# Loading order of the MLP weights in a decoder layer: the block that is added to comes first

## The chip, the cores and the metric

The kernel runs on one core of one Trainium2 chip. The core has a matmul engine (TensorE, PE in the profile, with PEld for its weight loads), a vector engine (VectorE, DVE), a scalar engine (ScalarE, ACT), GpSimd (POOL) and SyncE (SP). Each takes its instructions in the order in which they were written down and waits on semaphores for the others. PE accumulates in PSUM; everything else lies in SBUF. Transfers between HBM and SBUF are issued by SP or POOL and carried by 16 DMA engines. The metric is the device time of one execution in microseconds (us).

## The reference, cut to what matters

A hybrid layer: a chunked mLSTM and a sliding-window attention on one normalised input, an output projection, an MLP, a gated extra embedding and a last norm. 512 tokens, width 1024, float32. What the change touches is the MLP with its 4096 hidden features:

```python
u = rmsnorm(x, norm_mlp_g[i]) @ w_up[i]
x = x + jnp.square(jax.nn.relu(u)) @ w_down[i]
```

## The kernel before

**Arithmetic.** A float32 number is split into two parts of the type float32r: the high part is a rounded copy, made by ACT (a cast, L1318), and the low part is what the copy lost, made by DVE (a subtraction, L1321). A product is three matmuls, high by high, high by low and low by high. One pair of parts of a 128 x 1024 block of weights is called a form here; there are four buffers of each part (`wh`, `wl`), so a form waits until the product four forms earlier has been computed.

**Seven products for eight.** Most of the MLP is done as 2 x 2 blocks by Winograd's form of Strassen's method: seven block products, w1 to w7, and some sums of blocks. The weights of one such set are four blocks b11, b12, b21, b22 (for the down projection two of each, one for each half `kh` of the contracted features). The sums on the weights' side are made in place:

- t3 = b12 + b22. It is made by a transfer: b12 is loaded, and then POOL issues a second transfer of b22 from HBM that adds to the same buffer while it arrives (`add_to`, L1299). This is called the adding transfer. b22 is also loaded by itself.
- t2 = t3 - b11, written over b11 (DVE, L1559 in an up set, L1648 in the down projection), t4 = b21 - t2 over b21, t1 = b22 - t2 over b11 (DVE, L1563, L1564, L1648).

So b11 serves w1, then t2 takes its place for w6, then t1 for w5; t3 serves w7, b22 w3, and b21 first w2 and then, as t4, w4. The order of the products on PE is w1, w2, w6, w5, w7, w3, w4, in the first down projection w2 before w1.

**Order of the stages.** The first eight 128-row pieces of the up projection are computed plainly (`up_first`). Then follow: down 0; up set 2, up set 3, down 1; up set 4, up set 5, down 2; up set 6, up set 7, down 3. An up set (L1485 on) gives 512 hidden features, a down projection (L1592 on) takes 1024 of them. Between one stage and the next PE has no pause by itself: the first product of the next stage is written directly behind the last one of this stage.

**Results.** In an up set w2's sum plus a copy k1 of w1 becomes one quarter (called c11), w7's sum plus a copy becomes c22, w3's c12; these additions are DVE's L1544, followed by ACT's ReLU and square. Three accumulators X, Y, Z in PSUM are reused: w4 is written on X and must wait until c22 has read it. In a down projection DVE adds each finished accumulator to the residual stream `xk` (L1631); the last two of these additions read Y, which the next up set's w2 overwrites.

**Two rings of buffers.** Raw blocks land in two rings of four buffers each, `wr` and `wd`. A load may start when the block that had this buffer four loads earlier in the same ring has had its last reader (`ring_free`), and loads of a ring start in order. Even up sets use `wr`, odd ones `wd`. A down projection uses both: `wr` for b11 and b21, `wd` for b12 and b22.

**The plan.** `Plan.run` (L51 on) writes down the order of all engines' work from the tuples of `Plan.add`: engine, cost, dependencies, and `late`, the time from the task's end until another engine can use its result. Backwards from PE's order each task gets a due time; forwards the task that can begin first is written next, the earlier due one on a tie. Costs and `late` are estimates in us; for a load on SP 1.3 and 2.5, for an adding transfer on POOL 1.2 and 5.0. They decide nothing but the order. The loads of a set are created in the order b11, b21, b12, b22 (L1491, L1593), the adding transfer behind w1.

Of the kernel before, what the change touches and what calls it, by code (L numbers as in the profile page):

```python
# [13 lines left out]
ALU = mybir.AluOpType  # L14
# [67 lines left out]
def block_kernel(  # L82
# [30 lines left out]
    nc = tc.nc  # L113
# [247 lines left out]
    e1, _ = early_part(1)  # L361
# [75 lines left out]
    with tc.issue_after(copied.ins):  # L437
        xn2, _ = norm(2)
# [3 lines left out]
    for m in range(NT):  # L442
        if m == 1:
            columns(2, xn2)
        elif m == 2:
            with tc.issue_after(on_scalar):
                xn, _ = norm(3)
            _, on_vector = columns(3, xn)
# [4 lines left out]
        t = sp.tile([P, 256], F32, tag="vs", bufs=4, name=nm("vs"))  # L453
# [146 lines left out]
    for m in range(NT):  # L600
        t = tp_.tile([P, NH * (DV + 2)], F32R, tag="tk", bufs=4, name=nm("vm")).rearrange("p (h d) -> p h d", h=NH)
# [313 lines left out]
    for u in range(16):  # L915
# [4 lines left out]
        if u % 4 == 3:  # L920
            kp, n, _ = units[u]
# [104 lines left out]
    t2 = [None] * 8  # L1026
# [262 lines left out]
    plan = Plan(tc)  # L1289
    LO, HI, HALF_UP, HALF_DOWN = 1.15, 0.98, 1.45, 1.37  # L1290
    forms, ring, slots = [], {"wr": [], "wd": []}, {}

    def ring_free(tag):
        old = ring[tag]
        return old[-1:] + (slots["last", old[-4]] if len(old) > 3 else [])

    def add_to(t, src, user):

        return plan.add("POOL", 1.2, lambda: [nc.gpsimd.dma_start(out=slots[user], in_=src, accum_op=ALU.add)], [t], 5.0)  # L1299

    def load(tag, src, user):

        def go():
            slots[user] = (wr if tag == "wr" else wd)()
            return [nc.sync.dma_start(out=slots[user], in_=src)]

        t = plan.add("SP", 1.3, go, ring_free(tag), 2.5)
        ring[tag].append(t)
        slots["last", t] = []
        return t  # L1310
# [174 lines left out]
    def up_set(i, ready):  # L1485
# [2 lines left out]
        role[:] = [Y, Z, X]  # L1488
        tag = "wr" if i % 2 == 0 else "wd"
        name = [(i, n) for n in ("b11", "b21", "b12", "b22")]  # L1490
        l11, l21, l12, l22 = [load(tag, w_upb[4 * i - 8 + n], u) for u, n in zip(name, (0, 2, 1, 3))]  # L1491
        b11, b21, b12, b22 = name
        keep = {}

        def half(ps):
# [59 lines left out]

        begun_set = plan.add("none", 0, lambda: begin() or [], done_with.get("F", []) + done_with.get(("uf", i), []))
        w1 = prod(X, A11, b11, [l11], True, False, (done_with.get(id(X), []), []))
        t3 = add_to(l12, w_upb[4 * i - 8 + 3], b12)
        t2 = vec(LO, lambda: V.tensor_sub(slots[b11], slots[b12], slots[b11]), [t3, w1["lo"]])  # L1559
        w2 = prod(Y, A12, b21, [l21], True, True, (done_with.get(id(Y), []), []))  # L1560
        k1 = kept("k1", X, w1["use"], done_with.get("k1", []))
# [28 lines left out]
    uf_of = {}  # L1590

    def down(q, ready):  # L1592
        names = ("b11", "b21", "b12", "b22")  # L1593
        src = {
            (n, kh): ("wr" if i < 2 else "wd", w_down[q * 8 + 4 * kh + (0, 2, 1, 3)[i]], (q, n, kh, "d"))
            for i, n in enumerate(names)
            for kh in range(2)
        }
        ld = {k: load(*v) for k, v in src.items()}
        raw = lambda n, kh: slots[q, n, kh, "d"]  # L1600
        X, Y, Z = role
        Gb = G1_
# [43 lines left out]

        n2 = range(2)
        sub = lambda o, a, b: lambda: V.tensor_sub(raw(*o), raw(*a), raw(*b))  # L1648
        w1, w2, w6, w5, t1, t2, t3, t4 = [[None] * 2 for _ in range(8)]
        more = None  # L1650
        for kh in range(2):
            if not q:
                w2[kh], u2 = half(X, A12, "b21", kh, ld["b21", kh], True, True)
            w1[kh], u1 = half(Gb, A11, "b11", kh, ld["b11", kh], q == 0, False)
            t3[kh] = add_to(ld["b12", kh], w_down[q * 8 + 4 * kh + 3], (q, "b12", kh, "d"))
            t2[kh] = vec(LO, sub(("b11", kh), ("b12", kh), ("b11", kh)), [t3[kh], w1[kh]["lo"]])
            if q == 3 and kh == 1:
                more = acc(Gb, 1, 0, u1)
            if q:
                w2[kh], u2 = half(X, A12, "b21", kh, ld["b21", kh], True, True)  # L1660
# [266 lines left out]
```

## Time and profile before

| what | us |
|---|---|
| three runs, median (lowest to highest) | 879.85 (876.97 to 879.88) |
| the profiled execution, time | 878.63 |
| its span, from the first to the last instruction | 876.8 |
| stretch before `up_first` (0 to 488) | 488.0, PE busy 485.9 |
| `up_first` (488 to 526) | 38.0, PE busy 38.0 |
| down 0 to down 3 (526 to 816) | 290.0, PE busy 278.1, DVE busy 251.8 |
| embedding gate and last norm (816 to the end) | 60.8, PE busy 53.7 |

Busy PE time takes the modelled ends of overlapping matmuls, so a pause of PE is some 0.16 us longer between the starts of two matmuls than the idle time that a row gives in brackets. In the rows of the timeline the columns are: start, duration, engine, line, operation, output<-inputs by the program's names with buffer numbers left out, shape, count; in square brackets the idle time of the engine before it and what ended it. SPq and POOLq are the issuing of transfers. `xk<-psp` is an addition to the residual stream, `k<-psp,k` one of c11, c22, c12, `wl<-wr,wh` a low part, `wr<-wr,wr` or `wr<-wd,wr` a sum of blocks.

### The profile page before, as it was taken

The numbers are of one execution on the slowest core, as the hardware profiler recorded it, in microseconds if no ns is written. First come the engines' busy times: TensorE is split into PE (matmuls) and PEld (weight loads), VectorE is DVE, ScalarE is ACT, GpSimd is POOL, SyncE is SP. The second block draws the span as 40 slices with busy tenths as digits, with TensorE's granted clock in tenths as the row PEclk, the third lists the DMA queues.
The fourth block names the chain that finished last, engine by engine and source line by source line (L and its number), as shares of the span: only waits on it lengthen the run. The fifth ranks groups of instructions, "written<-read, shape, count | busy, mean of one in ns | idle before, by whom it ended". The sixth has DMA issues, their size and how long they took to land.

```text
span 876.8 us, 12755 instructions
## 1 busy us (share of the span) xinstructions
PE 855.7 (98%) x4854; PEld 739.6 (84%) x4854; DVE 716.9 (82%) x1028; ACT 522.1 (60%) x893; POOL 58.6 (7%) x89
## 2 busy tenths in 40 slices
PE   9999999999999999999999999999999998999996
PEld 7888789998877778888888887899889888987886
DVE  7898978774788889677896888799969996999657
ACT  6776656554676677844343766277427743764743
POOL 3221111000000000000020000000000000010000
PEclk9999999999999999999999999999999999999998
DMA  8677236435122165663243450825253545443402
GB/s 285 210 195 273 96 123 214 163 127 192 49 96 73 61 228 217 211 254 135 73 97 120 121 166 25 216 97 144 91 150 120 121 145 118 144 123 104 159 1 96
DMA packets 37391, 123.60 MB, mean 141 GB/s; under 512 B 5197, under 2 KB 5197, under 8 KB 37330
## 3 DMA queue, kind: packets, MB, share of 16 engines
q1 hardware_dynamic: 28578, 95.77, 31.9%
q0 software_dynamic: 8608, 26.75, 12.3%
q8 instruction: 38, 0.62, 0.3%
q10 hardware_dynamic: 144, 0.26, 0.1%
q14 instruction: 23, 0.19, 0.1%
HBM read 106.51 MB, written 11.54 MB: 135 GB/s over the span
## 4 chain that ended last, share of the span: by engine, by line
PE 63%; DVE 14%; issue 9%; DMA 8%; ACT 5%; POOL 0%; POOLq 0%; ACTq 0%; DVEq 0%
PE psg L222 25%; PE psa L222 10%; PE psp L1333 7%; PE psg L1333 6%; PE psp L222 6%; DVE wl L1321 5%; DMA wr<-in_w_upb 4%; PE pst L222 4%; DMA wd<-in_w_down 2%; DVE wr L1648 2%; DVE xk L1631 2%; ACT wh L1318 1%; PE psp L1167 1%; PE pst L899 1%; DMA wr<-in_w_down 1%
## 5 line engine op out<-in xcount | busy, mean ns | idle before, releaser
L183 ACT CAST wh<-wr 128x1024 fp32r<-128x1024 f32 x87 | 91.7, 1055 | 87.2 <-PE psg L222 29.9
L184 DVE TENSOR_TENSOR wl<-wr,wh 128x1024 fp32r<-128x1024 f32 x87 | 106.1, 1221 | 42.7 <-ACT wh L183 42.4
L1333 PE MATMUL psp<-x,wh 128*128 128x256 f32 x672 | 123.2, 286 | 8.8 <-DVE xk L1631 5.7
L1318 ACT CAST wh<-wr 128x1024 fp32r<-128x1024 f32 x67 | 69.5, 1049 | 92.0 <-DVE wr L1648 34.0
L1333 PEld LDWEIGHTS psp<-x,wh 128*128 128x128 f32 x672 | 106.1, 194 | 10.2 <-issue 6.2
L1333 PE MATMUL psp<-wh,uf 128*128 128x512 f32 x336 | 105.8, 390 | 0.3 <-ACT wh L1318 0.3
L1333 PE MATMUL psp<-x,wl 128*128 128x256 f32 x336 | 95.7, 285 | 0.0
L1321 DVE TENSOR_TENSOR wl<-wr,wh 128x1024 fp32r<-128x1024 f32 x67 | 81.1, 1221 | 6.0 <-ACT wh L1318 6.0
L222 PE MATMUL psg<-h,wh 128*128 128x512 f32 x256 | 80.1, 393 | 0.0
L1333 PEld LDWEIGHTS psp<-wh,uf 128*128 128x128 f32 x336 | 63.1, 188 | 14.3 <-ACT wh L1318 1.0
L1333 PE MATMUL psp<-wl,uf 128*128 128x512 f32 x168 | 65.9, 392 | 2.8 <-DVE wl L1321 2.8
L1333 PEld LDWEIGHTS psp<-x,wl 128*128 128x128 f32 x336 | 65.2, 194 | 0.0
L222 PEld LDWEIGHTS psg<-h,wh 128*128 128x128 f32 x256 | 46.9, 188 | 8.9
L222 PE MATMUL psg<-h,wl 128*128 128x512 f32 x128 | 50.1, 391 | 0.0
L1321 DVE TENSOR_TENSOR wl<-wd,wh 128x1024 fp32r<-128x1024 f32 x37 | 44.8, 1220 | 1.3 <-ACT wh L1318 1.1
L1318 ACT CAST wh<-wd 128x1024 fp32r<-128x1024 f32 x37 | 38.0, 1049 | 11.4 <-PE psp L1333 11.4
L1333 PEld LDWEIGHTS psp<-wl,uf 128*128 128x128 f32 x168 | 31.5, 188 | 10.6 <-DVE wl L1321 4.3
L222 PE MATMUL psg<-yb,wh 128*128 128x512 f32 x128 | 40.2, 394 | 0.2 <-issue 0.2
L1351 DVE TENSOR_TENSOR uf<-F,uf 128x512 fp32r<-128x512 f32 (+2 forms) x30 | 34.2, 1149 | 7.5 <-ACT uf L1350 7.2
L1631 DVE SCALAR_TENSOR_TENSOR xk<-psp,r,xk 128x512 f32<-128x512 f32 x42 | 30.0, 747 | 11.2 <-PE psp L1333 11.0
L1333 PE MATMUL psg<-wh,uf 128*128 128x512 f32 x112 | 36.5, 389 | 0.0
L222 PE MATMUL psg<-ya,wh 128*128 128x512 f32 x112 | 34.9, 391 | 0.0
(401 smaller groups left out, 2150.7 us busy)
## 6 DMA issues: line engine op xcount, KB each, us to landing
wr<-in_w_down SPq DMA_DIRECT2D x16, 512.0 KB, 4.5
wd<-in_w_down SPq DMA_DIRECT2D x16, 512.0 KB, 4.3
wr<-in_w_upb SPq DMA_DIRECT2D x12, 512.0 KB, 3.5
wd<-in_w_upb SPq DMA_DIRECT2D x12, 512.0 KB, 4.4
wr<-in_w_qsw SPq DMA_DIRECT2D x8, 512.0 KB, 4.3
gd<-gr POOLq DMA_DIRECT2D x8, 512.0 KB, 3.5
wr<-in_w_qkml SPq DMA_DIRECT2D x8, 512.0 KB, 3.2
wr<-in_w_b SPq DMA_DIRECT2D x8, 512.0 KB, 3.5
```

The lines of the kernel that those rows point to most:

```text
L183: A.copy(dst[0], src)
L184: last_low[0] = V.tensor_sub(dst[1], src, r32(dst[0]))
L222: last_mm[0] = T.matmul(ps, l, r, start=first and i == 0, stop=last and i == len(ops) - 1, skip_group_check=parts)
L899: T.matmul(o[HALF[ab], :], v[:, c : c + 64], w[:, ab * 512 : (ab + 1) * 512], start=j == 0, stop=j == len(terms) - 1)
L1167: T.transpose(ps[:, c, m * P : (m + 1) * P], xk[m][:, (k + c) * P : (k + c + 1) * P], ident)
L1318: return [A.copy(parts[0], slots[user])]
L1321: return [V.tensor_sub(parts[1], slots[user], r32(parts[0]))]
L1333: yield T.matmul(ps, l, r, start=first and j == 0, stop=last and j == len(ops) - 1, skip_group_check=True)
L1351: return vec(n / 512 * 0.54 + 0.06, lambda: V.tensor_sub(dst()[1], src(), r32(dst()[0])), [h])
L1631: return V.scalar_tensor_tensor(o, ps[t] if ps is Gb else ps[:, t, :], f, o, ALU.mult, ALU.add)
L1648: sub = lambda o, a, b: lambda: V.tensor_sub(raw(*o), raw(*a), raw(*b))
```

## The change

Four edits, all in the functions above.

- In an up set the loads are created in the order b12, b11, b21, b22, and the adding transfer directly behind b12's load instead of behind w1.
- In a down projection the loads are created in the order b12, b11 for each half, then b21, b22 for each half, with the adding transfer directly behind b12's load. b11 and b12 now lie in `wr`, b21 and b22 in `wd`.
- The plan reckons 1.9 and 3.0 for a load (1.3 and 2.5 before).
- The plan reckons a `late` of 6.0 for an adding transfer (5.0 before).

```diff
@@ add_to, load
-        return plan.add("POOL", 1.2, lambda: [nc.gpsimd.dma_start(out=slots[user], in_=src, accum_op=ALU.add)], [t], 5.0)
+        return plan.add("POOL", 1.2, lambda: [nc.gpsimd.dma_start(out=slots[user], in_=src, accum_op=ALU.add)], [t], 6.0)
...
-        t = plan.add("SP", 1.3, go, ring_free(tag), 2.5)
+        t = plan.add("SP", 1.9, go, ring_free(tag), 3.0)
@@ up_set
-        l11, l21, l12, l22 = [load(tag, w_upb[4 * i - 8 + n], u) for u, n in zip(name, (0, 2, 1, 3))]
         b11, b21, b12, b22 = name
+        l12 = load(tag, w_upb[4 * i - 8 + 1], b12)
+        t3 = add_to(l12, w_upb[4 * i - 8 + 3], b12)
+        l11, l21, l22 = [load(tag, w_upb[4 * i - 8 + n], u) for u, n in ((b11, 0), (b21, 2), (b22, 3))]
...
-        t3 = add_to(l12, w_upb[4 * i - 8 + 3], b12)
@@ down
-        src = {
-            (n, kh): ("wr" if i < 2 else "wd", w_down[q * 8 + 4 * kh + (0, 2, 1, 3)[i]], (q, n, kh, "d"))
-            for i, n in enumerate(names)
-            for kh in range(2)
-        }
-        ld = {k: load(*v) for k, v in src.items()}
+        ld, t3 = {}, [None] * 2
+        for two in (("b12", "b11"), ("b21", "b22")):
+            for kh in range(2):
+                for n in two:
+                    src = w_down[q * 8 + 4 * kh + ("b11", "b12", "b21", "b22").index(n)]
+                    ld[n, kh] = load("wr" if n < "b2" else "wd", src, (q, n, kh, "d"))
+                    if n == "b12":
+                        t3[kh] = add_to(ld[n, kh], w_down[q * 8 + 4 * kh + 3], (q, n, kh, "d"))
...
-            t3[kh] = add_to(ld["b12", kh], w_down[q * 8 + 4 * kh + 3], (q, "b12", kh, "d"))
```

PE's order stays what it was. Three places where the order of others moves follow; the lines of the code below L1488 are one to two higher in the changed kernel.

**SP, the loads of up sets 2 and 3** (they stand behind those of down 0). Before, in this order: set 2's b11 and b21, set 3's b11, b21, b12 and b22, and last set 2's b12 and b22:

```order
L1305 DMA wr_5388<-in_w_upb 128x1024
L1305 DMA wr_5442<-in_w_upb 128x1024
L1305 DMA wd_5448<-in_w_upb 128x1024
L1305 DMA wd_5467<-in_w_upb 128x1024
L1305 DMA wd_5476<-in_w_upb 128x1024
L1305 DMA wd_5490<-in_w_upb 128x1024
L1305 DMA wr_5510<-in_w_upb 128x1024
L1305 DMA wr_5521<-in_w_upb 128x1024
```

Now set 2's b12, b11, b21 and b22, then set 3's in the same order:

```order
L1305 DMA wr_5444<-in_w_upb 128x1024
L1305 DMA wr_5463<-in_w_upb 128x1024
L1305 DMA wr_5473<-in_w_upb 128x1024
L1305 DMA wr_5493<-in_w_upb 128x1024
L1305 DMA wd_5506<-in_w_upb 128x1024
L1305 DMA wd_5516<-in_w_upb 128x1024
L1305 DMA wd_5538<-in_w_upb 128x1024
L1305 DMA wd_5551<-in_w_upb 128x1024
```

Set 2's b12 moved from the seventh place to the first, and its b11 from the first to the second. It is the same at sets 4 and 5 and at sets 6 and 7.

**POOL, the adding transfers** from up set 3's and 2's to those of down 1. Before, set 3's came first, and those of down 1 went to `wd`:

```order
L1299 DMA wd_5476<-in_w_upb 128x1024
L1299 DMA wr_5510<-in_w_upb 128x1024
L1299 DMA wd_5875<-in_w_down 128x1024
L1299 DMA wd_5962<-in_w_down 128x1024
L1299 DMA wd_6223<-in_w_upb 128x1024
```

Now set 2's comes first, and down 1's go to `wr`:

```order
L1299 DMA wr_5444<-in_w_upb 128x1024
L1299 DMA wd_5506<-in_w_upb 128x1024
L1299 DMA wr_5659<-in_w_down 128x1024
L1299 DMA wr_5725<-in_w_down 128x1024
L1299 DMA wr_6190<-in_w_upb 128x1024
```

The buffer that down 1's first adding transfer waits for is thereby one of up set 2 (`wr`) and no longer one of up set 3 (`wd`).

**DVE, where down 0 ends and up set 2 begins.** Before: w1's low part, two additions to `xk` from Z (psp_4967), w2's low part, the first addition from Y (psp_4966), t2 (L1559), the second from Y, t4 (L1563), w6's low part, t1 (L1564), c11 (L1544), w5's low part:

```order
L1321 TENSOR_TENSOR wl_5531<-wr_5388,wh_5530 128x1024
L1631 SCALAR_TENSOR_TENSOR xk_4211<-psp_4967,r_4964,xk_4211 128x512
L1631 SCALAR_TENSOR_TENSOR xk_4212<-psp_4967,r_4964,xk_4212 128x512
L1321 TENSOR_TENSOR wl_5551<-wr_5442,wh_5550 128x1024
L1631 SCALAR_TENSOR_TENSOR xk_4209<-psp_4966,r_4964,xk_4209 128x512
L1559 TENSOR_TENSOR wr_5388<-wr_5510,wr_5388 128x1024
L1631 SCALAR_TENSOR_TENSOR xk_4210<-psp_4966,r_4964,xk_4210 128x512
L1563 TENSOR_TENSOR wr_5442<-wr_5442,wr_5388 128x1024
L1321 TENSOR_TENSOR wl_5592<-wr_5388,wh_5591 128x1024
L1564 TENSOR_TENSOR wr_5388<-wr_5521,wr_5388 128x1024
L1544 TENSOR_TENSOR k_982_5620<-psp_4966,k_982_5620 128x512
L1321 TENSOR_TENSOR wl_5636<-wr_5388,wh_5635 128x1024
```

Now (t2 is L1560, t4 L1564, t1 L1565, the additions to `xk` L1633):

```order
L1321 TENSOR_TENSOR wl_5527<-wr_5463,wh_5526 128x1024
L1560 TENSOR_TENSOR wr_5463<-wr_5444,wr_5463 128x1024
L1633 SCALAR_TENSOR_TENSOR xk_4211<-psp_4967,r_4964,xk_4211 128x512
L1321 TENSOR_TENSOR wl_5549<-wr_5473,wh_5548 128x1024
L1564 TENSOR_TENSOR wr_5473<-wr_5473,wr_5463 128x1024
L1633 SCALAR_TENSOR_TENSOR xk_4212<-psp_4967,r_4964,xk_4212 128x512
L1633 SCALAR_TENSOR_TENSOR xk_4209<-psp_4966,r_4964,xk_4209 128x512
L1321 TENSOR_TENSOR wl_5569<-wr_5463,wh_5568 128x1024
L1633 SCALAR_TENSOR_TENSOR xk_4210<-psp_4966,r_4964,xk_4210 128x512
L1565 TENSOR_TENSOR wr_5463<-wr_5493,wr_5463 128x1024
L1321 TENSOR_TENSOR wl_5610<-wr_5463,wh_5609 128x1024
L1321 TENSOR_TENSOR wl_5628<-wr_5444,wh_5627 128x1024
```

t2 now stands directly behind w1's low part, four places further ahead, with both additions from Y behind it; t4 stands ahead of them as well, and w6's low part between them. c11 moved behind the low parts of w5 and w7. In the down projections 1 to 3 DVE's order is unchanged.

More of the change, by code (lines that the diff above doesn't have):

```diff
@@ L1592, in down @@
     def down(q, ready):
-        names = ("b11", "b21", "b12", "b22")
-        src = {
-            (n, kh): ("wr" if i < 2 else "wd", w_down[q * 8 + 4 * kh + (0, 2, 1, 3)[i]], (q, n, kh, "d"))
-            for i, n in enumerate(names)
-            for kh in range(2)
-        }
-        ld = {k: load(*v) for k, v in src.items()}
+        ld, t3 = {}, [None] * 2
[6 more added lines that the diff above has]
+                        t3[kh] = add_to(ld[n, kh], w_down[q * 8 + 4 * kh + 3], (q, n, kh, "d"))
         raw = lambda n, kh: slots[q, n, kh, "d"]
@@ L1648, in down @@
         sub = lambda o, a, b: lambda: V.tensor_sub(raw(*o), raw(*a), raw(*b))
-        w1, w2, w6, w5, t1, t2, t3, t4 = [[None] * 2 for _ in range(8)]
+        w1, w2, w6, w5, t1, t2, t4 = [[None] * 2 for _ in range(7)]
         more = None
```

## The prediction

> **What bounds the kernel now.** The page's first table comes first:
>
> ```profile
> span 876.8 us, 12755 instructions
> PE 855.7 (98%) x4854; PEld 739.6 (84%) x4854; DVE 716.9 (82%) x1028; ACT 522.1 (60%) x893; POOL 58.6 (7%) x89
> ```
>
> The change removes no matmul, so PE's own work stays, and only its pauses can be had. The view of the waits, for PE between 485 and 820 us (the MLP, the only part that is edited), lists them all:
>
> ```profile
> PE psp L1333 <- DVE xk L1631: 5.7, 3, 2.3
> PE psp L1333 <- DVE k L1544: 3.2, 3, 1.3
> PE psp L1333 <- DVE wl L1321: 2.8, 4, 1.6
> PE psp L1333 <- ACT wh L1318: 0.3, 1, 0.3
> ```
>
> Eleven pauses, 12.0 us (total, count, longest). Each is really some 0.16 us longer from start to start: in the rows below, PE's last matmul begins at 568.77, its neighbours follow each other by 0.12, so the next could begin at 568.89; it begins at 570.45, 1.56 us late where the bracket says 1.40. With 11 x 0.16 the stock is **13.8 us**, 1.6% of the span. More than that the change can't bring.
>
> **First term: the pauses behind `xk`.** Rows of the timeline, DVE, PE and then ACT, where down 0 ends and up set 2 begins:
>
> ```profile
> 559.15 1.23 DVE L1321 TENSOR_TENSOR wl<-wr,wh 128x1024 fp32r<-128x1024 f32 x1
> 566.22 0.75 DVE L1631 SCALAR_TENSOR_TENSOR xk<-psp,r,xk 128x512 f32<-128x512 f32 x1 [2.90 <-PE psp L1333]
> 568.42 1.23 DVE L1559 TENSOR_TENSOR wr<-wr,wr 128x1024 f32<-128x1024 f32 x1 [1.45 <-DMA wr<-in_w_upb]
> 569.56 0.75 DVE L1631 SCALAR_TENSOR_TENSOR xk<-psp,r,xk 128x512 f32<-128x512 f32 x1
> 570.22 1.22 DVE L1563 TENSOR_TENSOR wr<-wr,wr 128x1024 f32<-128x1024 f32 x1
> 571.35 1.22 DVE L1321 TENSOR_TENSOR wl<-wr,wh 128x1024 fp32r<-128x1024 f32 x1
> 568.77 0.28 PE L1333 MATMUL psp<-x,wl 128*128 128x256 f32 x1
> 570.45 0.47 PE L1333 MATMUL psp<-x,wh 128*128 128x256 f32 x2 [1.40 <-DVE xk L1631]
> 558.06 1.06 ACT L1318 CAST wh<-wr 128x1024 fp32r<-128x1024 f32 x1 [1.66 <-PE psp L1333]
> 569.76 1.05 ACT L1318 CAST wh<-wr 128x1024 fp32r<-128x1024 f32 x1 [7.92 <-DVE wr L1559]
> 570.71 0.58 ACT L1529 COPY k<-psp 128x512 f32<-128x512 f32 x1
> ```
>
> PE waits for the second addition from Y (569.56 to 570.31). That addition was not slow: it stood behind t2, and t2 waited 1.45 us for the adding transfer, with DVE idle. So the releaser named on PE's row is a bystander; the cause is a transfer. Why is it late?
>
> ```profile
> 546.93 1.22 DVE L1321 TENSOR_TENSOR wl<-wd,wh 128x1024 fp32r<-128x1024 f32 x1
> 554.11 1.22 DVE L1321 TENSOR_TENSOR wl<-wr,wh 128x1024 fp32r<-128x1024 f32 x1
> 555.36 2.88 SPq L1305 DMA_DIRECT2D wr<-in_w_upb  x2
> 561.44 0.84 POOL L1299 DMA_DIRECT2D wr<-in_w_upb  x1 [4.18 <-DMA wr<-in_w_upb]
> DMA to landing us min/median/max: 3.3/4.3/6.4
> DMA to landing us min/median/max: 6.8/7.2/8.4
> ```
>
> (The last two lines are the sums of the views of one line, L1305 and L1299: all loads, and all adding transfers.) Set 2's b12 was third in its ring, so its buffer came free with the low part of down 0's w4, first half (554.11 to 555.33); issued at 555.36, it released POOL 6.1 us later, and the added block arrived about 568.3.
>
> After the change b12 is first and takes the buffer of down 0's b12, whose last reader is the low part of w7, first half: 546.93 to 548.15. Issue 548.2. The three loads behind it queue after it, so I take a load's 3.3 to 4.3 us and 0.6 for POOL's wake-up: POOL issues at 552.1 to 553.1, and with 6.8 to 7.2 the block is there between 558.9 and 560.3; with the longest of both rows, 548.2 + 6.4 + 0.6 + 8.4 = 563.6.
>
> Now the new DVE order, since t2 stands directly behind w1's low part, which ends at 560.38 (its cast at 558.06 waited for PE, so it does not move). From there until the first addition from Y come t2, an addition, w2's low part, t4, an addition: by the distances of starts above (569.56 - 568.42 = 1.14 for a large one, 570.22 - 569.56 = 0.66 for an addition) 3 x 1.14 + 2 x 0.66 = 4.74 us. The addition from Y can't begin before 566.22 anyway (PE). So t2 may begin as late as **561.48** without harm, and I have it at 560.4. Then first addition 566.22, w6's low part 566.88, second addition 568.02 to 568.77, PE 0.14 later (570.31 to 570.45): 568.91, against 568.89 wished. The pause is gone although w6's low part has been put between the additions; what is late next is k1 on ACT, behind the cast of t1: t1 568.68 to 569.91, cast and copy 1.05 + 0.58, so 571.6 against a wish for w6 at 568.89 + 24 x 0.12 = 571.8. Just hidden. Set 2's b11, issued first before and second now, arrives by 549.4 + 6.4 = 555.8 at worst, and is cast at 558.06; set 3's blocks start four buffers later and are needed 20 us later. The distances are the same at sets 4 and 6. Term: 5.7 + 3 x 0.16 = 6.2, less 0.2 for the ties: **6.0 us**.
>
> A page of the Trainium skill speaks against this mechanism as a whole: "DMA: Bandwidth & Descriptors", section "Anatomy of one DMA — SWDGE (gpsimd) path", gives a transfer issued by GpSimd about 2 us and its bytes over 436 GB/s, 3.2 us for 512 KB as an estimate. By that the block issued at 561.44 would have been there at 564.6, t2 would not have waited, and this term would be 0. The trace disagrees: none took under 6.8 us, and DVE's 1.45 us of waiting end with it.
>
> **Second term: the pauses behind `k`.** The same views where up set 3 ends:
>
> ```profile
> DVE wr L1648 <- DMA wd<-in_w_down: 3.5, 3, 1.2
> 597.25 0.85 POOL L1299 DMA_DIRECT2D wd<-in_w_down  x1 [34.97 <-DMA wd<-in_w_down]
> 602.19 1.22 DVE L1321 TENSOR_TENSOR wl<-wr,wh 128x1024 fp32r<-128x1024 f32 x1
> 604.56 1.23 DVE L1648 TENSOR_TENSOR wr<-wd,wr 128x1024 f32<-128x1024 f32 x1 [1.16 <-DMA wd<-in_w_down]
> 605.70 0.68 DVE L1544 TENSOR_TENSOR k<-psp,k 128x512 f32<-128x512 f32 x1
> 606.44 0.51 PE L1333 MATMUL psp<-x,wh 128*128 128x256 f32 x2 [1.20 <-DVE k L1544]
> ```
>
> Again DVE is held by a t2, that of down 1, and c22 behind it releases PE's w4 too late. Three such DVE waits make 3.5 us, three PE pauses 3.2 + 0.5 = 3.7. After the change down 1's b12 takes a `wr` buffer of set 2, free with the low part of its w7 (the first row; the second is set 3's w7, the third the cast of down 1's b21 for w2):
>
> ```profile
> 576.15 1.22 DVE L1321 TENSOR_TENSOR wl<-wr,wh 128x1024 fp32r<-128x1024 f32 x1
> 593.72 1.22 DVE L1321 TENSOR_TENSOR wl<-wd,wh 128x1024 fp32r<-128x1024 f32 x1
> 603.51 1.03 ACT L1318 CAST wh<-wr 128x1024 fp32r<-128x1024 f32 x1
> ```
>
> 577.4 + 6.4 + 0.6 + 8.4 = 592.8 at worst, ten us before t2's turn at 603.4. b21 pays for it: its first load now waits for set 3's w7 (until 594.94) and lands by 601.3 at worst, before the cast at 603.51; hidden. With DVE's idle 1.16 gone c22 would be 0.2 late at its old lead; in the up sets DVE starts t2, t4 and all behind them some 2.4 us earlier against PE, since the 2.90 and 1.45 us of idling now hold work, and part of that lead lasts. I take **3.5 us**.
>
> **Third term: the rest**, 2.8 + 0.3 + 5 x 0.16 = 3.9 us:
>
> ```profile
> 543.69 0.74 DVE L1631 SCALAR_TENSOR_TENSOR xk<-psp,r,xk 128x512 f32<-128x512 f32 x1
> 545.13 0.75 DVE L1631 SCALAR_TENSOR_TENSOR xk<-psp,r,xk 128x512 f32<-128x512 f32 x1 [0.70 <-PE psp L1333]
> 545.80 1.22 DVE L1321 TENSOR_TENSOR wl<-wr,wh 128x1024 fp32r<-128x1024 f32 x1
> 547.07 0.50 PE L1333 MATMUL psp<-wl,uf 128*128 128x512 f32 x1 [1.58 <-DVE wl L1321]
> 795.53 0.50 PE L1333 MATMUL psp<-wh,uf 128*128 128x512 f32 x1 [0.29 <-ACT wh L1318]
> 796.85 0.50 PE L1333 MATMUL psp<-wl,uf 128*128 128x512 f32 x1 [0.81 <-DVE wl L1321]
> ```
>
> The 1.58 lies in down 0, where DVE works without a break up to an addition that itself waits for PE; no transfer is in it and DVE's order there is unchanged. It stays. The others (two of 0.19 in downs 1 and 2, 1.1 in down 3; 2.1 us with the 0.16 each) are DVE behind on work, in downs that begin with c22 late. DVE gets its 1.16 to 1.25 us of idling back, but PE also arrives 1.3 us earlier; only the lead from the up sets is net, which I put at under 1 us at a down's start. That pays for the small pauses and half of down 3's: **1.3 us**. Bounds: 0 to 2.1.
>
> **The sum.** 6.0 + 3.5 + 1.3 = **10.8 us** against the profiled execution's 878.63 (its span of 876.8 and 1.8 around it): **867.8 us**. That execution lies 1.2 us under the median of 879.85; two of the three runs are at 879.9, one at 877.0.
>
> The plan's new numbers cost nothing by themselves; they only set the orders weighed above. In `up_first` PE has no pause before, and the blocks of down 0 come in other order into buffers freed at the same moments, 10 us or more before use. Behind the MLP the `wr` ring is freed earlier than before (b12 instead of b21).
>
> **The rivals.**
>
> *The adding transfer is later than a row says* (0.14). It used to run beside the two loads of 555.36, now beside seven that follow b12. If it comes at 563.6, the bound above, t2 is 2.1 us past 561.48 at each of three sets: 6.4 us of pauses, as much as before. Between nothing and that I take 1.1 each: gain 7.5, **871.1**; at the bound 874.2. For it: the loads' own times spread from 3.3 to 6.4, and no row has eight in a row. Against: the median adding transfer, 7.2, has company too. The Trainium skill's page "DMA: Bandwidth & Descriptors", section "SWDGE vs HWDGE vs iDMA", says that a DMA engine takes turns between GpSimd's queue and the others'; by that the loads behind it do slow it, which no row here separates.
>
> *DVE becomes the bound* (0.12). The table by stretches, from 526 to 816 (length, then PE, PEld, DVE):
>
> ```profile
> 526.00:816.00 290.00, 278.10 (x1684) 248.52 (x1682) 251.82 (x264) 161.57 (x196) 12.37 (x16) 0.99 0.44 126
> ```
>
> DVE is busy 251.8 of 290 us; with 10.8 us less the margin shrinks from 13% to 10%, and the pauses of the second and third term return behind the low parts: gain 6.0, **872.6**. Against: DVE idles 2.9 us at each set's start waiting for PE.
>
> *It doesn't do what it says* (0.05): b12's load is held in SP's queue by a load ahead of it, and t2 waits as before: **878.6**. Against: in SP's new order nothing stands ahead.
>
> *Slower* (0.06): t2 now stands ahead of two additions and w2's low part, so a late block holds them all. Each us past 561.48 costs a us at three sets; the change loses once these pauses eat the 10.8, from 3.6 us past it, a block landing 17 us after b12's issue at 548.2. The rows' longest add up to 15.4. At 5.5 us past: 878.6 - 10.8 + 16.5 = **884.3**.
>
> **How the numbers follow.** Forecast 0.63, rivals 0.14, 0.12, 0.05, 0.06. Within 0.5% (4.4 us, about what a measurement of this kernel can tell from no change) lies the third rival; the first two are faster by more. So faster 0.89, same 0.05, slower 0.06. Low end: the whole stock without the 1.74 of down 0, 12.1 us, and a run 1.7 lower as the lowest was: 864.9. High end: the first rival's bound with half a us of scatter, 874.7.
>
> **What would show it.** DVE's waits for an `in_w_upb` and an `in_w_down` transfer leave the list, and with them PE's waits for `xk` and `k`; a pause near 547 of 1.58 remains; t2 begins directly behind w1's low part near 560. Wrong if DVE waits at L1560 past 561.5, or if PE's total for low parts grows instead of falling.

## The result and the profile after

The kernel after takes **866.96 us** (median of 4, 866.5 to 867.42) where the kernel before, run beside it, takes 879.87 (876.97 to 880.15): a ratio of 0.9861, with a 95% interval of 0.9839 to 0.9882. The forecast was 867.8.

The page's first table, as of before:

```profile
span 865.3 us, 12748 instructions
PE 852.9 (99%) x4854; PEld 738.1 (85%) x4854; DVE 717.9 (83%) x1028; ACT 522.5 (60%) x893; POOL 57.7 (7%) x89
```

DVE does the same work as before (717.9 us, 716.9 then) in a span 11.5 us shorter. What PE waits for in the MLP (485 to 810 us) has shrunk to one group of the waits (total, count, longest), and in DVE's list of the same stretch no transfer is left:

```profile
PE psp L1333 <- DVE wl L1321: 2.4, 2, 1.6
```

Those two are the pauses that the third term spoke of, the 1.6 in down 0 and the 0.8 in down 3. How long the MLP takes is read from the starts of its first and last product's matmuls on the timeline, before and then after:

```profile
487.81 0.61 PE L1333 MATMUL psg<-x,wh 128*128 128x512 f32 x2
815.57 0.39 PE L1333 MATMUL psg<-wh,uf 128*128 128x512 f32 x1
```

```profile
488.46 0.61 PE L1333 MATMUL psg<-x,wh 128*128 128x512 f32 x2
804.03 0.39 PE L1333 MATMUL psg<-wh,uf 128*128 128x512 f32 x1
```

327.8 us have become 315.6: the edited part gained 12.2 us. It began 0.65 later, before anything that is edited, so clock times of after are compared with those of the prediction plus 0.65.

Where down 0 ends and set 2 begins, the timeline of after has the loads (SP's queue), the adding transfer (POOL) and DVE as follows (x4: four loads, the first at 538.71):

```profile
538.71 12.24 SPq L1305 DMA_DIRECT2D wr<-in_w_upb  x4
542.68 0.84 POOL L1299 DMA_DIRECT2D wr<-in_w_upb  x1 [32.36 <-DVE wl L1321]
537.46 1.22 DVE L1321 TENSOR_TENSOR wl<-wr,wh 128x1024 fp32r<-128x1024 f32 x1
559.79 1.22 DVE L1321 TENSOR_TENSOR wl<-wr,wh 128x1024 fp32r<-128x1024 f32 x1
561.04 1.23 DVE L1560 TENSOR_TENSOR wr<-wr,wr 128x1024 f32<-128x1024 f32 x1
566.86 0.75 DVE L1633 SCALAR_TENSOR_TENSOR xk<-psp,r,xk 128x512 f32<-128x512 f32 x1 [0.88 <-PE psp L1333]
567.53 1.22 DVE L1321 TENSOR_TENSOR wl<-wr,wh 128x1024 fp32r<-128x1024 f32 x1
568.66 0.75 DVE L1633 SCALAR_TENSOR_TENSOR xk<-psp,r,xk 128x512 f32<-128x512 f32 x1
```

t2 (561.04) stands directly behind w1's low part and waits for nothing. The first addition from Y, w6's low part and the second addition come at 566.86, 567.53 and 568.66, where the prediction has 566.22, 566.88 and 568.02, each plus 0.65. But the first load was issued at 538.71, not at 548.2 plus 0.65: set 2's b12 did not take the buffer of down 0's b12, but that of its b11, which comes free when w5's first low part ends (537.46 + 1.22 = 538.68). The pool gives out the buffer that was freed first; the plan's ring names another. In the kernel before both orders are the same for set 2, so its trace could not tell them apart. So the added block is there at 548.0 (5.4 us from the issue, the shortest of the adding transfers in this trace), 13 us before t2.

### The profile page after: what moved, and what is told of

Read it like the earlier page. It is cut to its first block, busy times and chain, and to the rows that moved or that the text cites. A ratio compares the mean times of both kernels' runs of the same rounds, so it can differ in the third digit from the quotient of the medians.

```text
span 865.3 us, 12748 instructions
## 1 busy us (share of the span) xinstructions
PE 852.9 (99%) x4854; PEld 738.1 (85%) x4854; DVE 717.9 (83%) x1028; ACT 522.5 (60%) x893; POOL 57.7 (7%) x89
## 4 chain that ended last, share of the span: by engine, by line
PE 80%; issue 8%; DVE 6%; DMA 3%; ACT 2%; SPq 0%; POOL 0%; POOLq 0%; DVEq 0%; ACTq 0%
PE psp L1333 25%; PE psg L222 23%; PE psa L222 9%; PE psg L1333 8%; PE psp L222 6%; PE pst L222 4%; DVE wl L1321 1%; DMA wr<-in_w_vsif 1%; PE psp L1167 1%; PE pst L899 1%; PE psa L829 1%; DMA wo<-in_w_out 1%; DVE wl L184 1%; PE psa L830 1%; DMA xk<-in_x 1%
## 5 line engine op out<-in xcount | busy, mean ns | idle before, releaser
L183 ACT CAST wh<-wr 128x1024 fp32r<-128x1024 f32 x87 | 91.6, 1054 | 86.7 <-PE psg L222 30.0
L184 DVE TENSOR_TENSOR wl<-wr,wh 128x1024 fp32r<-128x1024 f32 x87 | 106.0, 1220 | 42.3 <-ACT wh L183 42.1
L1333 PE MATMUL psp<-x,wh 128*128 128x256 f32 x672 | 121.3, 283 | 0.0
L1318 ACT CAST wh<-wr 128x1024 fp32r<-128x1024 f32 x59 | 60.5, 1047 | 65.4 <-DVE wr L1650 34.0
L1321 DVE TENSOR_TENSOR wl<-wr,wh 128x1024 fp32r<-128x1024 f32 x59 | 71.4, 1219 | 8.9 <-ACT wh L1318 6.7
L1318 ACT CAST wh<-wd 128x1024 fp32r<-128x1024 f32 x45 | 47.2, 1049 | 28.6 <-PE psp L1333 20.3
L1321 DVE TENSOR_TENSOR wl<-wd,wh 128x1024 fp32r<-128x1024 f32 x45 | 54.6, 1218 | 1.1 <-ACT wh L1318 1.1
L1351 DVE TENSOR_TENSOR uf<-F,uf 128x512 fp32r<-128x512 f32 (+2 forms) x30 | 34.2, 1149 | 10.2 <-ACT uf L1350 10.0
L1333 PE MATMUL psg<-x,wh 128*128 128x512 f32 x112 | 34.4, 389 | 0.0
```

What stands on the lines that cost most here:

```text
L183: A.copy(dst[0], src)
L184: last_low[0] = V.tensor_sub(dst[1], src, r32(dst[0]))
L1318: return [A.copy(parts[0], slots[user])]
L1321: return [V.tensor_sub(parts[1], slots[user], r32(parts[0]))]
L1333: yield T.matmul(ps, l, r, start=first and j == 0, stop=last and j == len(ops) - 1, skip_group_check=True)
L1351: return vec(n / 512 * 0.54 + 0.06, lambda: V.tensor_sub(dst()[1], src(), r32(dst()[0])), [h])
```

## The experiments

"Pauses" is the total of PE's list of waits in the MLP; "MLP" is the time between the starts of its first and its last matmul in the profiled execution, read as above. All medians are of 4 to 10 runs, the ratios those to the kernel before on the same chip.

| kernel | pauses, us | MLP, us | median, us | ratio (95%) |
|---|---|---|---|---|
| before | 12.0 | 327.8 | 879.87 | 1 |
| after | 2.4 | 315.6 | 866.96 | 0.9861 (0.9839 to 0.9882) |
| e1 up_set's edit alone | 5.6 | 319.4 | 870.71 | 0.9889 (0.9855 to 0.9922) |
| e2 down's edit alone | 3.1 | 316.5 | 867.55 | 0.9847 (0.9807 to 0.9888) |
| e3 after, b12 third in up sets | 1.4 | 315.4 | 867.25 | 0.9847 (0.9813 to 0.9881) |
| e4 after, two adding transfers | 2.4 | 315.5 | 866.92 | 0.9844 (0.9810 to 0.9877) |
| e5 numbers alone | 8.6 | 323.5 | 874.34 | 0.9915 (0.9887 to 0.9943) |
| e6 both edits, old numbers | 2.4 | 315.6 | 866.65 | 0.9826 (0.9787 to 0.9866) |
| e7 after, four adding transfers | 31.0 | 350.0 | 901.15 | 1.0219 (1.0178 to 1.0260) |
| e8 after, last split in pieces | 0 | 312.0 | 863.05 | 0.9788 (0.9753 to 0.9823) |
| e9 down's rings alone | 3.2 | 316.6 | 868.13 | 0.9878 (0.9861 to 0.9896) |
| e10 after, three adding transfers | 11.7 | 329.6 | 883.79 | 1.0051 (1.0030 to 1.0072) |
| e11 e8, b12 third in up sets | 1.2 | 314.3 | 865.25 | 0.9811 (0.9779 to 0.9843) |
| e12 after once more | 2.4 | 315.6 | 866.37 | 0.9829 (0.9797 to 0.9861) |

The kernel before has medians of 879.8 to 881.4 beside these kernels, and single runs from 875.4 to 888.0; most of the others scatter far less. So kernels are compared below by their pauses, by the length of their MLP and by their own medians.

### Which part of the change does it (e1, e2, e9, e3)

e1 is before with these lines in `up_set`:

```diff
-        l11, l21, l12, l22 = [load(tag, w_upb[4 * i - 8 + n], u) for u, n in zip(name, (0, 2, 1, 3))]
+        l12 = load(tag, w_upb[4 * i - 8 + 1], b12)
+        t3 = add_to(l12, w_upb[4 * i - 8 + 3], b12)
+        l11, l21, l22 = [load(tag, w_upb[4 * i - 8 + n], u) for u, n in ((b11, 0), (b21, 2), (b22, 3))]
...
-        t3 = add_to(l12, w_upb[4 * i - 8 + 3], b12)
```

> The kernel before with the edit of up_set alone (its b12 is loaded and added to first; the down projections and the plan's numbers stay). Theory on record (two separate causes): the pauses behind xk go (6.2 us between 485 and 820 us), those behind k stay (3 of them, 3.2 to 3.5 us as listed): about 6.0 us less than before, near 872 for a profiled execution. Rival (the pauses are one stock of DVE lag, which moves): the pauses behind xk go, but those behind k or behind the low parts grow by as much; under 3 us gained. By the trace of after, b12 of set 2 should be issued near 538.7, at the end of w5's first low part, not near 548.2 as the prediction has it.

e1's waits of PE:

```profile
PE psp L1333 <- DVE wl L1321: 3.2, 4, 1.6
PE psp L1333 <- DVE xk L1632: 1.8, 2, 1.0
PE psp L1333 <- ACT wh L1318: 0.6, 1, 0.6
```

e1's timeline at set 2: its last two loads (b21 and b22) on SP's queue, ACT's cast of b21, and the last addition behind it on DVE:

```profile
555.74 2.89 SPq L1305 DMA_DIRECT2D wr<-in_w_upb  x2
563.45 2.00 ACT L1318 CAST wh<-wr 128x1024 fp32r<-128x1024 f32 x2 [3.94 <-DMA wr<-in_w_upb]
569.39 0.74 DVE L1632 SCALAR_TENSOR_TENSOR xk<-psp,r,xk 128x512 f32<-128x512 f32 x1
```

Neither expectation fits. DVE waits for no transfer at all any more, not in the downs either, and the pauses behind `k` are gone too, since the plan, with an earlier t3, has written another order there (c22 stands ahead of down 1's t2). But at set 2 the late buffer has only passed to another block: b21 is third in the ring now, is issued at 555.74, where b12 was in before (555.36), and ACT waits 3.94 us for it. w2's low part, t4 and the additions are late with it, and PE waits 0.84 for the last one (569.39).

e2 is before with the rewritten head of `down` alone, and e9 is e2 with one more line, so that b12 is not ahead any longer. Against before e9 changes the rings; the loads of the two halves alternate and the adding transfer is created behind its load, as in the change:

```diff
-        for two in (("b12", "b11"), ("b21", "b22")):
+        for two in (("b11", "b12"), ("b21", "b22")):
```

> The kernel before with the edit of down alone (rings changed, b12 first there; up_set and the plan's numbers stay). Theory on record: the pauses behind k go (3.7 us), those behind xk (6.2 us) stay; near 875. Rival (what counts is when a buffer comes free, not the place in the set): with the new rings the wr buffers come free at w5 and w7 of down 0, so that even the third load, set 2's b12, can be issued near 549 instead of 555.4; with 4.3 to 6.4 us for the load, 0.6 for POOL and 5.4 to 8.6 for the adding transfer it lands between 559 and 564.6 against 561.5, and the pauses behind xk shrink from about 2 us each to between 0 and 3, near 0.5; near 870 to 871.

> The run with down's edit alone, with b12 behind b11 in down's `wr` ring instead of ahead of it: only the rings are changed (b11 and b12 in `wr`, b21 and b22 in `wd`), no block that takes an adding transfer is moved ahead of its set, and the numbers are those of before. Theory (the rings do it, through the time at which buffers come free): as the run with down's edit alone, 867.5, within 1 us; no pause behind k, at most 1 us behind xk. Rival (b12's place ahead in down does it): pauses behind k of 1 us each at the starts of downs 1 to 3 are back, 870 or more.

e2's waits, PE's and then DVE's one wait for a transfer:

```profile
PE psp L1333 <- DVE wl L1321: 2.4, 2, 1.6
PE psp L1333 <- DVE xk L1632: 0.7, 2, 0.5
...
DVE wr L1559 <- DMA wr<-in_w_upb: 2.5, 2, 1.6
```

e2's timeline at set 2, the adding transfer on POOL and t2 on DVE:

```profile
553.62 0.84 POOL L1299 DMA_DIRECT2D wr<-in_w_upb  x1 [44.91 <-DMA wr<-in_w_upb]
562.73 1.23 DVE L1559 TENSOR_TENSOR wr<-wr,wr 128x1024 f32<-128x1024 f32 x1 [0.90 <-DMA wr<-in_w_upb]
```

down's edit alone also removes the pauses of the up sets, which it does not touch, but for 0.7 us, and with 867.55 it is 0.6 us above the whole change. The rival of e2 holds, though its 870 to 871 was 2.5 us too much: what counts is when a buffer comes free. With b11 and b12 in one ring, the `wr` buffers come free at down's w5 and w7, and even as the third load b12 lands about when t2 has its turn; ACT waits for no load. e9 shows that it is the rings: its list of waits has the same two groups (2.4 and 0.8), no pause behind `k`, and 868.13 us. How the rings act is not separated: the planner, which reckons with the free buffers, puts t2 ahead of both additions from Y in e2 and e9 too, as in after, and no run has the new rings with the old order on DVE.

e3 puts b12 third in the up sets of the kernel after:

```diff
-        l12 = load(tag, w_upb[4 * i - 8 + 1], b12)
-        t3 = add_to(l12, w_upb[4 * i - 8 + 3], b12)
-        l11, l21, l22 = [load(tag, w_upb[4 * i - 8 + n], u) for u, n in ((b11, 0), (b21, 2), (b22, 3))]
+        l11, l21, l12, l22 = [load(tag, w_upb[4 * i - 8 + n], u) for u, n in ((b11, 0), (b21, 2), (b12, 1), (b22, 3))]
+        t3 = add_to(l12, w_upb[4 * i - 8 + 3], b12)
```

> The kernel after, with b12 third again in each up set (b11, b21, b12, b22), and all else as after. It tries the times that the prediction has for b12 (issue 548.2, POOL 552.1 to 553.1, landing 558.9 to 563.6) which the kernel after does not use. Theory (a limit: t2 may begin as late as 561.5, and past that each us costs a us): issue near 548.8, landing 559 to 564, so a pause behind xk of 0 to 2.5 at each of three sets; 0 to 3 us slower than after. Rival (only the place in the set counts): the pauses return as before, 2 us each, 6 us slower than after.

Its waits of PE:

```profile
PE psp L1333 <- DVE wl L1321: 1.4, 2, 0.8
```

Its timeline at set 2, the adding transfer and t2:

```profile
552.27 0.84 POOL L1299 DMA_DIRECT2D wr<-in_w_upb  x1 [41.20 <-DVE xk L1632]
563.97 1.22 DVE L1559 TENSOR_TENSOR wr<-wr,wr 128x1024 f32<-128x1024 f32 x1
```

POOL issues at 552.27 and the block lands at 560.08. The MLP of e3 begins 1.23 us later than that of before (489.04), so on the prediction's clock that is 551.0 and 558.9, the early end of the 558.9 to 560.3 that it had for b12. No pause comes of it: the early end of the prediction's timetable would have done as well. Here the planner, told of a later block, puts t2 behind two additions, so t2's start at 563.97 is no measure of the limit. It also orders down 0 otherwise, where 1.0 us of the listed pause is gone; the MLP is no shorter for it (315.4 against 315.6). Being first in the set is worth nothing that these runs can tell, once the rings and the numbers are the new ones.

### The plan's numbers (e5, e6)

e5 is before with the new numbers, e6 is after with the old ones (this diff the other way round):

```diff
-        return plan.add("POOL", 1.2, lambda: [nc.gpsimd.dma_start(out=slots[user], in_=src, accum_op=ALU.add)], [t], 5.0)
+        return plan.add("POOL", 1.2, lambda: [nc.gpsimd.dma_start(out=slots[user], in_=src, accum_op=ALU.add)], [t], 6.0)
...
-        t = plan.add("SP", 1.3, go, ring_free(tag), 2.5)
+        t = plan.add("SP", 1.9, go, ring_free(tag), 3.0)
```

> The kernel before with the plan's new numbers alone (2.5 to 3.0 and 1.3 to 1.9 for a load, 5.0 to 6.0 for an adding transfer); no load changes its place or its buffer. Theory on record (they cost and bring nothing by themselves): pauses behind xk and k as before, 12.0 us in the list of waits, within 2 us of it, and the time within 0.3% of before. Rival (knowing of longer transfers, the planner puts other work ahead of t2, and DVE's idling is used): the pauses behind xk and k shrink by 3 us or more without any new order of the loads.

> The kernel after with the old numbers in the plan: both edits of the loads, nothing else. Theory (the gain is the loads' and their buffers'): pauses as after, 2.4 us in the list of waits, time within 1 us of after. Rival (the numbers carry part): pauses behind xk or k of 1 us or more are back.

e5's waits of PE:

```profile
PE psp L1333 <- DVE wl L1321: 7.7, 9, 1.6
PE psp L1333 <- ACT wh L1318: 0.7, 1, 0.7
PE psg L1333 <- DVE wl L1321: 0.2, 1, 0.2
```

e5's timeline at set 2, DVE's two additions (x2) and t2:

```profile
566.09 1.41 DVE L1631 SCALAR_TENSOR_TENSOR xk<-psp,r,xk 128x512 f32<-128x512 f32 x2 [2.90 <-PE psp L1333]
567.76 1.23 DVE L1559 TENSOR_TENSOR wr<-wr,wr 128x1024 f32<-128x1024 f32 x1 [0.26 <-DMA wr<-in_w_upb]
```

The rival holds. With the longer transfers in its sums the planner puts both additions (566.09) ahead of t2 (567.76), and no load moves; t2 then waits 0.26 instead of 1.45. All pauses behind `xk` and `k` are gone, 8.9 us of them, but 5.5 us come back behind low parts, since t2 and what hangs on it are late. The MLP is 4.3 us shorter than that of before (323.5 against 327.8). The median is 7.0 us lower, but the median of before beside e5 lies itself 2.8 us above its profiled execution. In e6 the same numbers are worth nothing: 866.65 without them. The three parts are substitutes: in the MLP e1, e2 and e5 gain 8.3, 11.2 and 4.3 us, and the whole change 12.2; by the medians beside them 10.7, 13.8 and 7.0, and the whole change 12.9 (15.0 in e12).

### How much room, and the price past it (e4, e10, e7)

Further adding transfers of b22 go to the same buffer: in e4 one more in every up set (first line), in e7 three more in the even up sets alone (`add_to` issues four; in e10 three). In e7 and e10 DVE's order is that of after; in e4 t2 stands behind the two additions from Z (562.71 at set 2):

```diff
+        t3 = add_to(t3, w_upb[4 * i - 8 + 3], b12)
...
-        t3 = add_to(l12, w_upb[4 * i - 8 + 3], b12)
+        t3 = add_to(l12, w_upb[4 * i - 8 + 3], b12, 4 if i % 2 == 0 else 1)
```

> The kernel after, with b22 added twice in the up sets by a second adding transfer behind the first (t3 is then b12 + 2 b22, and the output is not the reference's). Theory (slack): in the kernel after the added block of set 2 is there at 548.0 and first read at 561.0; a second transfer of 5.4 to 8.6 us ends by 557, still 4 us early, so the time does not change (within 1 us) and no pause behind xk appears. Rival (traffic: the transfers slow the loads beside them, and the margin is narrow): loads or t2 come late and pauses of 1 us or more appear at sets 2, 4 and 6; 3 us or more slower.

> The kernel after, with b22 added four times over in the even up sets (t3 is then b12 + 4 b22, and the output is not the reference's); every engine's order but POOL's is that of after. Theory (the limit of 561.5 and the price of the rival on the other side, a us of pause for each us past it): by the distances of the run with two, 5.8 us, the fourth lands at 542.7 + 4 x 5.4 to 7.0, 564 to 571, and t2 begins 2.5 to 9 us past the limit at sets 2, 4 and 6; PE's pauses there are as long as t2 is late past 561.5, within 0.5 us; 8 to 27 us slower than after, near 885. Rival (DVE makes it up with its idling of 10%): pauses well under t2's lateness; under 5 us slower.

> The kernel after with b22 added three times in the even up sets (t3 is b12 + 3 b22, the output is not the reference's). Two things are asked. The law: the third adding transfer lands near 566 by the distances of the run with four (547.93 to 557.78 to 566.56), so t2 begins 4.5 to 6 us past 561.5 and PE pauses for that long at sets 2, 4 and 6, 13 to 18 us in all, each within 0.3 us of t2's lateness. The clock: if a pause of some us always costs slow matmuls behind it, the granted clock falls to about half for some 3 us after each of the three and adds some 1.5 us each, 4 to 5 in all, so 881 to 890; rival: it is chance or needs a longer pause, the stretches behind keep 1.0 and the time is after plus the pauses alone.

e4's time is that of after, and its list of waits too: one more transfer fits (at set 2 it lands at 557.6). For e7, PE's waits for the additions and DVE's for the transfers:

```profile
PE psp L1333 <- DVE xk L1633: 28.6, 3, 10.6
...
DVE wr L1560 <- DMA wr<-in_w_upb: 32.0, 3, 11.7
```

The timeline of e7 at set 2, POOL's four issues and then t2:

```profile
542.02 0.84 POOL L1299 DMA_DIRECT2D wr<-in_w_upb  x1 [32.39 <-DVE wl L1321]
547.93 0.85 POOL L1299 DMA_DIRECT2D wr<-in_w_upb  x1 [5.07 <-DMA wr<-in_w_upb]
557.78 0.85 POOL L1299 DMA_DIRECT2D wr<-in_w_upb  x1 [9.00 <-DMA wr<-in_w_upb]
566.56 0.84 POOL L1299 DMA_DIRECT2D wr<-in_w_upb  x1 [7.93 <-DMA wr<-in_w_upb]
...
572.10 1.23 DVE L1560 TENSOR_TENSOR wr<-wr,wr 128x1024 f32<-128x1024 f32 x1 [11.70 <-DMA wr<-in_w_upb]
```

w1's low part begins at 559.17 here, 0.02 later than in before, so the limit is 561.50. t2 is 10.60 us past it, and PE pauses for 10.56 + 0.16 = 10.72. Over the three sets DVE waits 32.0 and PE pauses 28.6 + 0.48 = 29.1: 0.97 us of each wait are free, where the prediction has 561.48 - 560.38 = 1.10. In e10 the same, waits first:

```profile
PE psp L1333 <- DVE xk L1633: 9.3, 3, 3.8
...
DVE wr L1560 <- DMA wr<-in_w_upb: 12.7, 3, 4.9
```

And t2 of set 2 on e10's timeline:

```profile
564.32 1.23 DVE L1560 TENSOR_TENSOR wr<-wr,wr 128x1024 f32<-128x1024 f32 x1 [3.63 <-DMA wr<-in_w_upb]
```

12.7 - 9.3 - 0.48 = 2.9, again 0.97 a set. So a us past the limit costs a us of pause; DVE's idle tenth doesn't make it up. The expected times were off all the same. In e7 the transfers beside the loads of sets 2 and 3 took longer than assumed (rows above: 9.85 and 8.8 us from one issue to the next, 5.9 without loads beside), and e7 is 34.2 us over after, of which the pauses are 29.1. In e10 the third transfer landed 2 us earlier than expected, with pauses of 2.6 to 3.9 instead of 4.5 to 6; its median of 883.79 lies in the 881 to 890 that the theory of the clock gave, but by luck: the pauses are 3 us or more shorter than that range assumes, and the profiled execution, 880.88, is the lowest of ten runs (up to 886.8); there is no trace of the other nine. What both profiled executions hold beyond the pauses is in the last section.

### What is left (e8, e11, e12)

e8 takes up the third term. In after, DVE at the start of down 3:

```profile
776.98 2.29 DVE L1351 TENSOR_TENSOR uf<-F,uf 128x2048 fp32r<-128x2048 f32 x1
779.18 1.22 DVE L1321 TENSOR_TENSOR wl<-wr,wh 128x1024 fp32r<-128x1024 f32 x1
...
781.57 1.23 DVE L1650 TENSOR_TENSOR wr<-wd,wr 128x1024 f32<-128x1024 f32 x1
782.71 1.40 DVE L1633 SCALAR_TENSOR_TENSOR xk<-psp,r,xk 128x512 f32<-128x512 f32 x2
784.03 2.35 DVE L1321 TENSOR_TENSOR wl<-wr,wh 128x1024 fp32r<-128x1024 f32 x2
```

The last split of the feature sums (776.98) delays w6's low part, t4, t1 and through them w5's second low part (784.03), for which PE waits. w6 and w5 need only two of its four sums. e8 splits these first, before the fourth sum is even made (for down 3 as shown, and in the same way in `up_first`, for down 0):

```diff
-        last = split_tasks(lambda: [t[:, 3 * 512 :] for t in uf_of[i]], lambda: flat(fs()), 2048, [s4])
-        done_with["F"] = [last]
+        p12, p0, p3 = sum_parts(i, fs, *feature_sums(fs, c21, a11, a22, a12))
+        done_with["F"] = [p12, p0, p3]
...
+    def sum_parts(i, fs, s3, s2, s4):
+        def piece(o, n, dep):
+            return split_tasks(
+                lambda: [t[:, (3 + o) * 512 : (3 + o + n) * 512] for t in uf_of[i]], lambda: flat(fs()[:, o : o + n]), n * 512, [dep]
+            )
+        return piece(1, 2, s2), piece(0, 1, s3), piece(3, 1, s4)
```

> The kernel after, with the last split of the feature sums (2048 wide) in three pieces: the two sums that w6 and w5 need first (1024 wide), then the other two by themselves (512 each). Theory (what is left in downs 0 and 3, 1.58 + 0.8 us in the list of waits and 3.9 from start to start, is a chain on DVE at a down's start: the last split, w6's low part, t4, t1, then w5's second low part): about 1.1 to 1.7 us of DVE work leave that chain, the pauses of downs 0 and 3 shrink by 1.5 to 3.5 us in all; near 864.5. Rival (the extra instructions on DVE and ACT, some 0.1 us each in eight sets, and the pieces end up between other work): no gain, or a new pause behind w7's or w3's sums; within 1 us of after.

In e8's down 3 the first piece and w5's second low part (the first of two, x2) stand so:

```profile
775.66 1.22 DVE L1351 TENSOR_TENSOR uf<-F,uf 128x1024 fp32r<-128x1024 f32 x1
...
779.80 2.35 DVE L1321 TENSOR_TENSOR wl<-wr,wh 128x1024 fp32r<-128x1024 f32 x2
```

The low part comes at 779.80 instead of 784.03. Of these 4.2 us the chain gives 1.6, inside the 1.1 to 1.7 expected; the rest is that PE itself is earlier (it begins that product at 781.54, in after at 785.30 with 1.09 of pause). PE's list of waits is empty. With 863.05 us (862.26 to 864.17) this version beats both kernels: 2.1% under before.

> The kernel after, unchanged, on the chip of the run beside it, so that the pieces can be told from the change itself: 866.5 to 867.5, with 3 to 4.5 us to the kernel in pieces if the chain on DVE was the cause of what is left; under 1.5 us if the earlier difference was the chip's.

> The kernel with the last split in pieces, and b12 third again in the up sets (what is left of the change is then down's order, its rings and the numbers). Theory (the place in the set is worth nothing once buffers come free at w5 and w7): as with the pieces alone, 863, within 1 us; no pause in the list of waits over 0.5 us. Rival (with no other pause left, the later t2 shows): pauses behind xk of 0.5 us or more at sets 2, 4 and 6, 865 or more.

e11 has e3's edit on top of e8's. e12 gives 866.37, so the pieces are worth 3.3 us. That run stood beside e11, on another chip than e8; against e6, which stood beside e8 and has the pauses of after, it is 3.6, and by the MLP's length 3.5 (315.57 and 312.05). e11 is 2.2 us above e8, where 1 was expected at most, for a reason that neither expectation had: the planner puts one of the 512 wide pieces ahead of the 1024 wide one in down 0, and PE waits there for the latter, 1.4 us of the 2.2 from start to start:

```profile
545.09 0.50 PE L1333 MATMUL psp<-wh,uf 128*128 128x512 f32 x1 [1.23 <-DVE uf L1351]
```

No pause behind `xk` is back. So the place in the set matters in e11 through the planner's order, not through the transfer.

## Why the prediction was right, and where it was not

**What bounds.** PE's pauses were the stock, and they were what went. The stock itself was mis-sized: 13.8 us leave out matmuls that run slowly behind one of the pauses (1.5 us, last section), so that the MLP could gain more than "the whole stock without the 1.74 of down 0". The sums below take each pause from start to start, as it stands on the timeline.

**First term, 6.0.** The three pauses behind `xk` (1.56, 2.16 and 2.42, together 6.14) are gone as forecast, and the slow matmuls with them: 7.6 in all. The limit for t2, the distances of the new DVE order and PE's price past the limit are right to within 0.15 us (561.04 and the rows behind it; e7, e10). The step that failed is "takes the buffer of down 0's b12 ... Issue 548.2": it was 538.71, since the buffer freed first is handed out. It didn't matter, as e3 with POOL at 552.27 shows. Nor is b12's first place, which the term names, what the gain hangs on: by itself it brings 8.3 of the 12.2 us in the MLP (e1), the rings in `down` by themselves 11.1 (e9), and beside the rings it adds nothing (e3).

**Second term, 3.5.** It brought 3.63 (1.36, 0.80 and 1.47), all of it. Its issue time fails by the step of the first term: down 1's first load is issued at 572.98, not at 577.4 plus 0.65, and that did not matter either. That DVE's freed time becomes a lead which covers c22 was argued from the up sets; the runs don't test it apart from the rest.

**Third term, 1.3.** This is the term that was mis-sized; it brought 0.91. The two pauses of 0.19 and the 0.29 have left the list: the first two (0.35 each from start to start) are gone, the third went from 0.45 to 0.24. But half of down 3's was to be paid by DVE's lead, and the 0.81 is unchanged:

```profile
785.30 0.50 PE L1333 MATMUL psp<-wl,uf 128*128 128x512 f32 x1 [0.81 <-DVE wl L1321]
```

The lead there grew by 0.2 us and no more: the last split of down 3 begins 12.30 us behind the down's first matmul (776.98 and 764.68), in before 12.51 (788.52 and 776.01). The term itself has the reason that is nearest, that PE arrives earlier by about what DVE gets back; no run tests it. The 1.58 of down 0 stayed as forecast (1.59). It was not beyond reach, however: e8 removes it.

**The numbers.** "The plan's new numbers cost nothing by themselves" is true beside the new loads (e6) and false alone: by themselves they gain 4.3 us in the MLP (e5).

**The rivals.** That the adding transfer slows beside loads is true (5.9 against 8.8 to 9.85 us in e7). In after it decided nothing, because the loads begin 10 us earlier than reckoned; in e2 and e9, where set 2's block took 9.0 us beside loads, it left 0.3 and 0.8 us of pause. DVE was not the bound: from 526 to 804.5 it is busy 252 of 278 us, and no pause came back. The slower case has its price right, a us for a us, but not its reach: from 548 the block would have to come 14 us later before PE noticed (13 until t2's turn and the 0.97 that are free), and e4 is no slower for one more transfer.

**The sum.** 10.8 was forecast for what measured 12.2 in the MLP: 10.68 of pauses (6.14, 3.63 and 0.91), in which the misses of the terms cancel, and 1.5 of slow matmuls, which the prediction put at nothing although the trace of before has them. The 0.65 by which the MLP began later took some of it back, so the profiled executions differ by 11.6 (878.63 and 867.06). That the time came within 0.9 us of 867.8 is in that part luck.

## What to carry to other kernels

When a wait for a transfer shows, ask first which buffer the load gets and when that buffer's last reader is done: here a change of rings in one stage freed buffers for the next stage, and the order inside a set, which gives 8.3 of the 12.2 us by itself, added nothing to that. A planner that is told too short a transfer writes an order in which others stand behind the late one; longer costs alone gave 4.3 us. Before counting parts of a change as a sum, run them singly: these three replace each other, 23.8 us when added up against 12.2 together.

## What was not expected of the hardware

A pause of PE can cost more than its length. The granted clock in stretches behind pauses: in before, behind the three of 1.40, 2.00 and 2.27 us, and then in e10 behind those of 2.49, 3.76 and 3.03 us (length of the stretch, then PE, PEld, DVE, ACT, POOL, then the clock):

```profile
570.40:573.60 3.20, 3.15 (x26) 3.18 (x27) 3.17 (x3) 0.89 (x2) 0.00 (x0) 1.00 0.00 0
653.08:657.10 4.02, 4.02 (x21) 4.02 (x22) 3.34 (x3) 1.38 (x3) 0.00 (x0) 0.58 0.00 0
736.94:741.00 4.06, 4.06 (x34) 4.06 (x35) 3.95 (x4) 1.43 (x3) 0.00 (x0) 1.00 0.00 0
```

```profile
571.86:576.00 4.14, 4.14 (x22) 4.14 (x23) 2.75 (x3) 2.47 (x3) 0.00 (x0) 0.59 0.00 0
656.05:660.00 3.95, 3.95 (x23) 3.95 (x24) 2.56 (x3) 2.48 (x3) 0.00 (x0) 0.66 0.00 0
739.54:743.50 3.96, 3.96 (x21) 3.96 (x22) 2.56 (x3) 2.48 (x3) 0.00 (x0) 0.60 0.00 0
```

In before 21 matmuls run in 4 us behind the second pause and 34 behind the third, longer one. In e10 it happens all three times, and in e7 too.

The matmuls follow each other there by 0.21 instead of 0.12 us for 3.1 to 3.6 us, which costs some 1.5 us each time. e10's MLP is 14.1 us longer than that of after (329.63 and 315.57): 9.8 of pauses and 4.3 of this; e7's is 34.5 longer (350.03), with 29.1 of pauses and 5.4, in slow stretches of 2.9, 5.6 and 4.2 us. The Trainium skill's page "TensorE: Matmul & The Clock Gate", section "Part 1: The HAM clock gate (the "warmup" mystery)", has the clock fall to half after an idle window of about 3.4 us and come back after as much work. The length of the stretches in before and e10 agrees, two of e7's are longer; that pauses of 2.00 and 2.49 us set it off does not agree. Why 2.27 us did not, no run here separates. It would also explain why the kernel before scatters between 875 and 888 us with a mean clock of 0.986 to 0.999, and the kernel after, whose longest pause is 1.6, by less than 2 us at 0.997 to 0.999 (e12 included). Of the runs of before those above 883 us have 0.992 or less and those under 878 have 0.996 or more, but one of 881.64 has 0.999; it was not tested.
